# Experts 4 to 6 stored from 96 partitions in 16 KB runs, and the last expert's output moved into a used weight slot

## The chip, the cores and the metric

The kernel runs on one core of one Trainium2 chip. The metric is the device time of one execution in microseconds (us); smaller is better. The engines are named as in the profile: PE is TensorE, DVE is VectorE, ACT is ScalarE, POOL is GpSimd and SP is SyncE. PEld is PE's weight load. The core has 16 DMA engines, which move data between HBM (device memory) and SBUF (on-chip memory of 128 partitions) for whichever engine issues the transfer. The kernel issues transfers from two engines: POOL, whose queue the profile calls q0, and SP, whose queue it calls q1.

## The reference

Eight experts each apply a two-layer network with a ReLU to 256 rows of their own. Inputs and output are float32.

```python
n_experts, capacity, hidden, expert_hidden = 8, 256, 512, 2048
# x: [8, 256, 512]   w1: [8, 512, 2048]   w2: [8, 2048, 512]
def reference(x, w1, w2):
    h = np.matmul(x, w1)
    h = np.maximum(h, 0)
    return np.matmul(h, w2).astype(np.float32)
```

The two weights of one expert are 4 MB each, so 64 MB of weights are read once; x is 4 MB and the output is 4 MB (512 KB for each expert).

## The kernel before, in words

**Loads.** All weights are loaded by POOL (line 204), in the order of the list `loads`: w1 and w2 of experts 0 and 1 together, of 2 and 3 together, then w1 of 4 and 5 together, and after that w2 of 4 and 5 and both weights of 6 and 7 one by one. The last w2 comes in two pieces, of 1280 KB and 768 KB in bfloat16. The loads convert float32 to bfloat16 on the way. There are four slots for w1 and four for w2 (`NS = 4`), so expert 4 uses the slots of expert 0, and so on; POOL waits for PE to be done with a slot before it issues the load that refills it. Everything on q0 is worked off in the order of issue, and each weight transfer lands tens of microseconds after it was issued.

**Start.** x comes in two parts: its first half through SP into `out_sb` (which holds no output yet) and its second half through POOL. PE transposes x in 64 steps (`xt_ps`), and DVE and ACT copy the transposed blocks out of PSUM into `xT` (`copy_xt`, lines 223 and 227): one copy for the columns of experts 0 to `QE` - 1 (the "early" ones, whose rows are put into another order, see below) and one for the rest (the "late" ones). `QE` is 4.

**Experts.** For each expert PE makes 64 matmuls of the first layer in four groups into two PSUM tiles (`h_ps`); ACT applies the ReLU and writes bfloat16 (`hT`, line 269). Then 32 matmuls of the second layer go into one PSUM tile `o_ps` of two halves. DVE copies `o_ps` to `out_sb`. PE may not write `o_ps` again before that, so DVE counts up the semaphore `c_o` twice for each expert, and PE takes one count near the end of each half of the next expert's first layer.

**Outputs of experts 0 to 3.** The rows of these experts are ordered so that 32 partitions hold one expert, eight rows of 512 numbers each. DVE copies `o_ps` in four pieces of 32 partitions x 1024 numbers (line 244), each onto the 32 partitions of its expert. `out_sb` then holds on each of 128 partitions a run of 16 KB that is also 16 KB in one piece in HBM.

**Outputs of experts 4 to 7.** DVE copies the two halves as they are, 128 partitions x 512 numbers (line 255); the second half of the last expert is copied by ACT (line 275). A partition then holds 4 KB for each expert, and 4 KB is what lies in one piece in HBM.

**Stores.** There are three. POOL waits until DVE is done with expert 6 (`s_event`) and until the piece of 1280 KB of the last w2 has landed (`landed[-2]`), and then issues the store of experts 4 to 6 (line 207: 1536 KB, 128 partitions x 3 runs of 4 KB) and that of experts 0 to 3 (line 210: 2048 KB, 128 runs of 16 KB). SP waits for both copies of the last expert (`v_last`) and issues its store (line 166: 512 KB, 128 runs of 4 KB). The kernel ends when all have landed.

Of the kernel before, what the change touches and what calls it, by code (L numbers as in the profile page):

```python
# [8 lines left out]
FP32 = mybir.dt.float32  # L9
# [7 lines left out]
def kernel(  # L17
# [7 lines left out]
    nc = tc.nc  # L25
    P = 128
    E, C, H = x.shape
    F = w1.shape[2]
    MC = C // P
# [3 lines left out]
    R = E * C // P  # L33
# [20 lines left out]
    out_v = out.rearrange("e (p mo) k -> p e (mo k)", mo=MC)  # L54
# [4 lines left out]
    def allot(name, shape, dtype):  # L59
        nonlocal free  # L60
        places[name] = free
        t = nc.alloc_sbuf_tensor_at(name, shape, dtype, offset=free)
        free += math.prod(shape[1:]) * mybir.dt.size(dtype)
        return t


    out_sb = allot("out_sb", [P, E, MC, H], FP32)
    w1_sb = allot("w1_sb", [P, NS, K1 * F], BF16)
    w2_sb = allot("w2_sb", [P, NS, K2 * H], BF16)
    xT = allot("xT", [P, K1, MC, E * P], BF16)  # L70
    hT = allot("hT", [P, K2, C], BF16)
    identity = allot("identity", [P, P], BF16)
    W1_AT, W2_AT, XT_AT = places["w1_sb"], places["w2_sb"], places["xT"]
# [4 lines left out]
    xt_ps = [nc.alloc_psum_tensor(f"xt_ps{i}", [P, R // MC, P], BF16) for i in range(MC)]  # L78
    h_ps = [nc.alloc_psum_tensor(f"h_ps{i}", [P, GJ * C], FP32) for i in range(UG)]
    o_pair = nc.alloc_psum_tensor("o_ps", [P, MC * H], FP32)  # L80
    o_ps = [o_pair[:, i * H:(i + 1) * H] for i in range(MC)]
# [3 lines left out]
    def sem(name):  # L85
        s = nc.alloc_semaphore(name)
        sems.append(s)
        return s

    d_last, d_pool = sem("d_last"), sem("d_pool")  # L90
# [7 lines left out]
    s_event, s_cast, s_stored = sem("s_event"), sem("s_cast"), sem("s_stored")  # L98
    s_pe, v_last = sem("s_pe"), sem("v_last")
# [10 lines left out]
    def after_outputs(e, halves):  # L110
        return s_pe, K1 * MC + e * (NG + MC) + NG + halves


    c_h, c_o, c_w1, c_w2 = sem("c_h"), sem("c_o"), sem("c_w1"), sem("c_w2")
# [15 lines left out]
    for w, es, h, _ in loads:  # L130
        s = d_half if h else d_w[w, es[0] % NS]
# [4 lines left out]

    QE = 4
    G = P // QE
    out_q = out_sb[:, :QE].rearrange("p e m h -> p (e m h)")
    out_qv = out[:QE].rearrange("e (p s) k -> (e p) (s k)", s=QE * MC)  # L140

    x_head = out_sb[:, :HEAD // MC].rearrange("p e m h -> p (e m h)")

# [17 lines left out]
    sp = nc.sync  # L161
    for i, (w, es, h, n) in enumerate(loads):
        sp.wait_ge(*landed[i])
        sp.sem_inc((c_w1, c_w2)[w - 1], n * len(es) if w == 2 else len(es))
    sp.wait_ge(v_last, MC)
    sp.dma_start(
        out_v[:, E - 1, :], out_sb[:, E - 1].rearrange("p m h -> p (m h)")
    ).then_inc(d_last, 16)
    sp.sem_inc(s_stored, 1)
    take(sp, d_last, 16)  # L170

# [1 line left out]
    pool = nc.gpsimd  # L173
# [5 lines left out]
        out=identity[:],  # L179
# [7 lines left out]
    for i, (w, es, h, n) in enumerate(loads):  # L187
# [10 lines left out]
        e, ne, at_slot = es[0], len(es), es[0] % NS  # L198
# [3 lines left out]
        else:  # L202
            src, dst = w1_v[:, e:e + ne, :], w1_sb[:, at_slot:at_slot + ne, :]
        pool.dma_start(dst, src).then_inc(landed[i][0], 16)  # L204
    pool.wait_ge(s_event, 3)
    pool.wait_ge(*landed[-2])
    pool.dma_start(  # L207
        out_v[:, QE:E - 1, :], out_sb[:, QE:E - 1].rearrange("p e m h -> p e (m h)")
    ).then_inc(d_pool, 16)
    pool.dma_start(out_qv, out_q).then_inc(d_pool, 16)  # L210
    pool.wait_ge(s_stored, 1)
    pool.wait_ge(d_pool, 48)
    used = [s.num for s in sems[1:]]
# [4 lines left out]


    def copy_xt(copy, ko, m):  # L220
        split = QE * C // R
        early, late = xT[:, ko, m, :QE * P], xT[:, ko, m, QE * P:]
        copy(  # L223
            early.rearrange("k (e g i hi) -> k hi g e i", e=QE, g=QE, hi=2),
            xt_ps[m][:, :, :split].rearrange("k (hi g) (e i) -> k hi g e i", hi=2, e=QE),
        )
        return copy(  # L227
            late.rearrange("k (ep r2) -> k ep r2", r2=R // MC),
            xt_ps[m][:, :, split:].rearrange("k r2 ep -> k ep r2"),
        )  # L230


    dve = nc.vector
# [3 lines left out]
    for ko in range(K1):  # L237
        dve.wait_ge(*after_transposes(ko * MC + 1))
        copy_xt(dve.tensor_copy, ko, 0).then_inc(c_xt[0])
    dve.sem_inc(c_o, MC)  # L240
    for e in range(QE):
        dve.wait_ge(*after_outputs(e, MC))
        for g in range(QE):
            cp = dve.tensor_copy(  # L244
                out_q[e * G:(e + 1) * G, g * MC * H:(g + 1) * MC * H],
                o_pair[g * G:(g + 1) * G, :],
            )
            if g >= QE - MC:
                cp.then_inc(c_o)
    for e in range(QE, E):  # L250
        for m in range(MC):
            if e == E - 1 and m == 1:
                break
            dve.wait_ge(*after_outputs(e, m + 1))
            cp = dve.tensor_copy(out_sb[:, e, m, :], o_ps[m])  # L255
            cp.then_inc(v_last if e == E - 1 else c_o)
        if e == E - 2:
            dve.drain().then_inc(s_event)


    act = nc.scalar
    act.sem_inc(c_xt[1], 1)
    for ko in range(K1):
        act.wait_ge(*after_transposes(ko * MC + 2))
        copy_xt(act.copy, ko, 1).then_inc(c_xt[1])
# [6 lines left out]
                mybir.ActivationFunctionType.Relu,  # L272
            ).then_inc(c_h)
    act.wait_ge(*after_outputs(E - 1, MC))
    act.copy(out_sb[:, E - 1, 1, :], o_ps[1]).then_inc(v_last)  # L275

# [50 lines left out]
    n = MC * (R // MC)  # L329
# [47 lines left out]
    lo, hi = bank  # L377
# [129 lines left out]
```

## Time and profile before

| | |
|---|---|
| median of 3 runs | 178.95 us (178.81 to 178.97) |
| the profiled execution, its own time | 178.98 us |
| its span, from the first to the last instruction or transfer | 177.7 us |
| PE busy | 128.1 us, 72% of the span |
| DVE busy, ACT busy | 31.6 us, 39.3 us |
| HBM read and written | 71.30 MB, 4.19 MB |

The profile is of one execution. Its own time is 1.28 us more than its span; times inside it are counted from the span's start. "Landing" of a transfer is the time from its issue until its semaphore shows that all of it has arrived. In the line of transferred GB/s, bytes are counted as they are written, so a load that converts float32 to bfloat16 shows half of what it reads.

### The profile page before, as it was taken

The page shows a single profiled execution, that of the slowest core. Times are in us where ns is not written, and L with a number is a line of the kernel's source. Part 1 is how long each engine was busy: PE and PEld are TensorE (multiplying, and loading weights), DVE is VectorE, ACT ScalarE, POOL GpSimd, SP SyncE. Part 2 cuts the span into 40 slices and gives each one's busy share as a digit, 9 for nine tenths or more (in the row PEclk, how much of TensorE's full clock was granted, in tenths as well). Part 3 has the DMA queues.
Part 4 walks back from the last instruction along what each step waited for, and adds up shares of the span by engine and source line. Part 5 has one row for each costly group of instructions (what it writes and reads, how often), then busy time and mean ns, then how long its engine had stood idle before and what let it go on. Part 6 is the DMA issues. An engine that isn't in the chain of part 4 may idle for free. (4 is left out here: it accounts for less than half of the span.)

```text
span 177.7 us, 2092 instructions
## 1 busy us (share of the span) xinstructions
PE 128.1 (72%) x832; PEld 89.4 (50%) x832; DVE 31.6 (18%) x32; ACT 39.3 (22%) x42; POOL 10.0 (6%) x21
## 2 busy tenths in 40 slices
PE   0008620793039989989069989989999999979980
PEld 0007520592013587488024885686497488459530
DVE  0054420000000180082000640280020020020010
ACT  2002520054000044025100242044035026005310
POOL 3400010000000002010000101200000000000200
PEclk9999999999756999999858999999999999999998
DMA  5999989989999999999999999999999999999998
GB/s 201 358 212 232 236 184 229 236 188 225 236 196 218 236 196 218 236 203 210 236 203 210 236 207 207 236 207 207 236 207 207 236 207 207 236 200 203 286 440 347
DMA packets 3488, 40.90 MB, mean 230 GB/s; under 512 B 288, under 2 KB 288, under 8 KB 928
## 3 DMA queue, kind: packets, MB, share of 16 engines
q0 software_dynamic: 3056, 38.27, 96.4%
q1 hardware_dynamic: 432, 2.62, 3.8%
HBM read 71.30 MB, written 4.19 MB: 425 GB/s over the span
## 5 line engine op out<-in xcount | busy, mean ns | idle before, releaser
L305 PE MATMUL o_ps<-w_sb,hT 128*128 x256 | 61.0, 399 | 16.7 <-PEq L102 16.7
L305 PE MATMUL h_ps<-xT,w_sb 128*128 x512 | 61.2, 279 | 11.8 <-PEq L102 11.8
L305 PEld LDWEIGHTS h_ps<-xT,w_sb 128*128 x512 | 57.4, 145 | 16.6 <-issue 14.1
L269 ACT ACTIVATE hT<-h_ps 128x1024 bf16<-128x1024 f32 x32 | 32.8, 1024 | 109.2 <-PE h_ps L305 109.2
L305 PEld LDWEIGHTS o_ps<-w_sb,hT 128*128 128x128 bf16 x256 | 25.5, 102 | 49.4 <-issue 23.0
L244 DVE COPY out_sb<-o_ps 32x1024 f32<-32x1024 f32 x16 | 19.5, 1220 | 75.8 <-PE o_ps L305 75.6
L305 PE MATMUL xt_ps<-identity,w_sb 128*128 128x128 bf16 x64 | 7.6, 312 | 15.8 <-PEq L102 15.8
L305 PEld LDWEIGHTS xt_ps<-identity,w_sb 128*128 x64 | 6.5, 147 | 16.6 <-issue 16.6
L255 DVE COPY out_sb<-o_ps 128x512 f32<-128x512 f32 x7 | 4.6, 687 | 49.2 <-PE o_ps L305 49.2
L204 POOL DMA_DIRECT2D w_sb<-in_w_dram x12 | 7.3, 615 | 103.9 <-PE h_ps L305 59.7
L223 ACT COPY xT<-xt_ps 128x512 bf16<-128x512 bf16 x4 | 2.9, 719 | 16.2 <-PE xt_ps L305 16.2
L235 DVE CAST w_sb<-out_sb 128x4096 bf16<-128x4096 f32 x1 | 2.3, 2295 | 10.4 <-DMA out_sb<-in_x_dram 10.4
L223 DVE COPY xT<-xt_ps 128x512 bf16<-128x512 bf16 x4 | 2.9, 730 | 5.9 <-PE xt_ps L305 5.9
L207 POOL DMA_DIRECT2D out_dram<-out_sb x1 | 0.8, 754 | 49.1 <-DMA w_sb<-in_w_dram 49.1
L227 DVE COPY xT<-xt_ps 128x512 bf16<-128x512 bf16 x4 | 2.7, 674 | 0.0
L227 ACT COPY xT<-xt_ps 128x512 bf16<-128x512 bf16 x4 | 2.4, 588 | 0.0
L275 ACT COPY out_sb<-o_ps 128x512 f32<-128x512 f32 x1 | 0.6, 586 | 5.9 <-PE o_ps L305 5.9
L223 ACT ACT_TABLE_LOAD x1 | 1.3, 1283 | 2.5 <-PEq L159 2.5
L174 POOL DMA_DIRECT2D w_sb<-in_x_dram x1 | 0.7, 650 | 2.5 <-POOLq L159 2.5
L210 POOL DMA_DIRECT2D out_dram<-out_sb x1 | 0.6, 572 | 0.0
L178 POOL TENSOR_SCALAR_AFFINE_SELECT identity<-identity 128x128 bf16<-128x128 bf16 x1 | 0.3, 282 | 0.2 <-POOL identity L175 0.2
L175 POOL MEMSET identity<- 128x128 bf16 x1 | 0.2, 223 | 0.0
(4 smaller groups left out, 0.4 us busy)
## 6 DMA issues: line engine op xcount, KB each, us to landing
w_sb<-in_w_dram POOLq DMA_DIRECT2D x5, 4096.0 KB, 46.3
w_sb<-in_w_dram POOLq DMA_DIRECT2D x5, 2048.0 KB, 50.4
out_sb<-in_x_dram SPq DMA_DIRECT2D x2, 1024.0 KB, 7.0
out_dram<-out_sb POOLq DMA_DIRECT2D x1, 2048.0 KB, 11.0
out_dram<-out_sb POOLq DMA_DIRECT2D x1, 1536.0 KB, 6.8
w_sb<-in_w_dram POOLq DMA_DIRECT2D x1, 1280.0 KB, 49.6
w_sb<-in_x_dram POOLq DMA_DIRECT2D x1, 1024.0 KB, 9.9
w_sb<-in_w_dram POOLq DMA_DIRECT2D x1, 768.0 KB, 52.7
```

The costliest lines, as they stand in the source:

```text
L174: pool.dma_start(x_sb[:, HEAD * H:], x_v[:, HEAD * H:]).then_inc(d_pool, 16)
L204: pool.dma_start(dst, src).then_inc(landed[i][0], 16)
L207: pool.dma_start(out_v[:, QE:E - 1, :], out_sb[:, QE:E - 1].rearrange("p e m h -> p e (m h)")).then_inc(d_pool, 16)
L210: pool.dma_start(out_qv, out_q).then_inc(d_pool, 16)
L223: copy(early.rearrange("k (e g i hi) -> k hi g e i", e=QE, g=QE, hi=2), xt_ps[m][:, :, :split].rearrange("k (hi g) (e i) -> k hi g e i", h ...
L227: return copy(late.rearrange("k (ep r2) -> k ep r2", r2=R // MC), xt_ps[m][:, :, split:].rearrange("k r2 ep -> k ep r2"),)
L235: dve.tensor_copy(x_sb[:, :HEAD * H], x_head).then_inc(s_cast)
L244: cp = dve.tensor_copy(out_q[e * G:(e + 1) * G, g * MC * H:(g + 1) * MC * H], o_pair[g * G:(g + 1) * G, :],)
L255: cp = dve.tensor_copy(out_sb[:, e, m, :], o_ps[m])
L269: act.activation(hT[:, g * GJ:(g + 1) * GJ, :].rearrange("p a c -> p (a c)"), h_ps[g % UG][:], mybir.ActivationFunctionType.Relu,).then_in ...
L275: act.copy(out_sb[:, E - 1, 1, :], o_ps[1]).then_inc(v_last)
L305: return pe.add_instruction(inst)
```

## The change

The 16 KB runs are extended from the first four to the first seven experts (`QA = 7`).

- DVE copies the outputs of experts 4 to 6 in four pieces of 32 x 1024 each, as it did those of 0 to 3, onto partitions 0 to 95 and behind the run of experts 0 to 3. Partitions 96 to 127 stay empty there. The two counts of `c_o` are given after the second and the fourth piece (before: after the third and the fourth), for all seven experts.
- `copy_xt` treats the columns of seven experts as early and those of the last one as late.
- POOL's two stores trade places: experts 0 to 3 first, now behind `landed[-2]` and a `s_event` that DVE gives after expert 3, then experts 4 to 6 behind a second `s_event` that DVE gives after expert 6. The latter is 96 runs of 16 KB on 96 partitions, in place of 384 runs of 4 KB on 128.
- The last expert's output goes to `last_sb`, which lies where the first w1 slot is (that of experts 0 and 4).

```diff
     QE = 4
     G = P // QE
-    out_q = out_sb[:, :QE].rearrange("p e m h -> p (e m h)")
-    out_qv = out[:QE].rearrange("e (p s) k -> (e p) (s k)", s=QE * MC)
+    QA = E - 1
+    out_q = out_sb.rearrange("p e m h -> p (e m h)")
+    out_qv = out.rearrange("e (p s) k -> (e p) (s k)", s=QE * MC)
+    RUN = QE * MC * H
+    last_sb = nc.alloc_sbuf_tensor_at("last_sb", [P, MC, H], FP32, offset=W1_AT)
...
-    pool.wait_ge(s_event, 3)
     pool.wait_ge(*landed[-2])
-    pool.dma_start(
-        out_v[:, QE:E - 1, :], out_sb[:, QE:E - 1].rearrange("p e m h -> p e (m h)")
-    ).then_inc(d_pool, 16)
-    pool.dma_start(out_qv, out_q).then_inc(d_pool, 16)
+    for first in range(0, QA, QE):
+        n = (min(first + QE, QA) - first) * G
+        at_run = first // QE * RUN
+        pool.wait_ge(s_event, 3 + first // QE)
+        pool.dma_start(
+            out_qv[first * G:first * G + n, :], out_q[:n, at_run:at_run + RUN]
+        ).then_inc(d_pool, 16)
...
-    for e in range(QE):
+    for e in range(QA):
         dve.wait_ge(*after_outputs(e, MC))
         for g in range(QE):
+            at_run = e // QE * RUN + g * MC * H
             cp = dve.tensor_copy(
-                out_q[e * G:(e + 1) * G, g * MC * H:(g + 1) * MC * H],
+                out_q[e % QE * G:(e % QE + 1) * G, at_run:at_run + MC * H],
                 o_pair[g * G:(g + 1) * G, :],
             )
-            if g >= QE - MC:
+            if g % MC == MC - 1:
                 cp.then_inc(c_o)
-    for e in range(QE, E):
-        for m in range(MC):
-            if e == E - 1 and m == 1:
-                break
-            dve.wait_ge(*after_outputs(e, m + 1))
-            cp = dve.tensor_copy(out_sb[:, e, m, :], o_ps[m])
-            cp.then_inc(v_last if e == E - 1 else c_o)
-        if e == E - 2:
+        if e in (QE - 1, QA - 1):
             dve.drain().then_inc(s_event)
+    dve.wait_ge(*after_outputs(E - 1, 1))
+    dve.tensor_copy(last_sb[:, 0, :], o_ps[0]).then_inc(v_last)
...
-    act.copy(out_sb[:, E - 1, 1, :], o_ps[1]).then_inc(v_last)
+    act.copy(last_sb[:, 1, :], o_ps[1]).then_inc(v_last)
```

On POOL, the end of its program stood like this before (a name before the arrow is written, the one behind it is read; w_sb are the weight slots, d_w2_3 is the semaphore of `landed[-2]`):

```order
L204 DMA w_sb<-in_w_dram 128x8192 [waits s_pe] x5
L204 DMA w_sb<-in_w_dram 128x5120 [waits s_pe]
L204 DMA w_sb<-in_w_dram 128x3072
L207 DMA out_dram<-out_sb 128x3x1024 [waits d_w2_3,s_event]
L210 DMA out_dram<-out_sb 128x4096
L216 ISA [waits d_pool,s_stored]
```

And it stands like this with the change:

```order
L205 DMA w_sb<-in_w_dram 128x8192 [waits s_pe] x5
L205 DMA w_sb<-in_w_dram 128x5120 [waits s_pe]
L205 DMA w_sb<-in_w_dram 128x3072
L211 DMA out_dram<-out_sb 128x4096 [waits s_event,d_w2_3]
L211 DMA out_dram<-out_sb 96x4096 [waits s_event]
L219 ISA [waits d_pool,s_stored]
```

The store of experts 0 to 3 has moved ahead of that of 4 to 6, and the latter has 96 runs of 4096 numbers instead of 128 x 3 runs of 1024 and a wait of its own.

On DVE, the end of its program, from expert 2 on, stood like this before (o_ps is the PSUM tile of the second layer):

```order
L244 COPY out_sb<-o_ps 32x1024 [waits s_pe]
L244 COPY out_sb<-o_ps 32x1024 x3
L244 COPY out_sb<-o_ps 32x1024 [waits s_pe]
L244 COPY out_sb<-o_ps 32x1024 x3
L255 COPY out_sb<-o_ps 128x512 [waits s_pe] x7
```

And from expert 4 on it stands like this with the change:

```order
L248 COPY out_sb<-o_ps 32x1024 [waits s_pe]
L248 COPY out_sb<-o_ps 32x1024 x3
L248 COPY out_sb<-o_ps 32x1024 [waits s_pe]
L248 COPY out_sb<-o_ps 32x1024 x3
L248 COPY out_sb<-o_ps 32x1024 [waits s_pe]
L248 COPY out_sb<-o_ps 32x1024 x3
L257 COPY last_sb<-o_ps 128x512 [waits s_pe]
```

Six of the seven copies of 128 x 512 have become twelve of 32 x 1024, with one wait for each expert instead of one for each half.

## Rows read from the trace of the kernel before

**Rows 1.** The page: busy time, DMA in 40 slices, queues, bytes.

```profile
PE 128.1 (72%) x832; PEld 89.4 (50%) x832; DVE 31.6 (18%) x32; ACT 39.3 (22%) x42; POOL 10.0 (6%) x21
...
DMA  5999989989999999999999999999999999999998
...
q0 software_dynamic: 3056, 38.27, 96.4%
q1 hardware_dynamic: 432, 2.62, 3.8%
HBM read 71.30 MB, written 4.19 MB: 425 GB/s over the span
```

**Rows 2.** Chain that ended last: start us, us, what.

```profile
158.14 0.04 issue
158.18 7.31 PE h_ps L305 x64
165.49 6.97 PE o_ps L305 x32
172.46 0.02 issue
172.48 0.59 ACT out_sb L275
```

**Rows 3.** Timeline, end: start us, us, engine, line; [idle before <-releaser].

```profile
157.05 1.29 DVE L255 COPY out_sb<-o_ps 128x512 f32<-128x512 f32 x2 [12.79 <-PE o_ps L305]
...
158.18 7.31 PE L305 MATMUL h_ps<-xT,w_sb 128*128 x64 [0.95 <-PEq L102]
...
164.70 0.75 POOL L207 DMA_DIRECT2D out_dram<-out_sb  x1 [49.12 <-DMA w_sb<-in_w_dram]
...
165.45 0.57 POOL L210 DMA_DIRECT2D out_dram<-out_sb  x1
...
173.10 0.35 SPq L166 DMA_DIRECT2D out_dram<-out_sb  x1
```

**Rows 4.** Transfers by issue: engine, count, KB each, us from issue to landing.

```profile
out_dram<-out_sb POOLq DMA_DIRECT2D x1, 2048.0 KB, 11.0
out_dram<-out_sb POOLq DMA_DIRECT2D x1, 1536.0 KB, 6.8
...
w_sb<-in_w_dram POOLq DMA_DIRECT2D x1, 768.0 KB, 52.7
out_dram<-out_sb SPq DMA_DIRECT2D x1, 512.0 KB, 4.5
```

**Rows 5.** Line 204, the weight loads: first and last issue, time to landing.

```profile
L204 POOL DMA_DIRECT2D w_sb<-in_w_dram x12: 528/554/733, 4.5 to 115.0; - x12
...
DMA to landing us min/median/max: 27.7/50.0/66.6
```

**Rows 6.** Four stretches; the last three columns: granted clock, DMA share, GB/s.

```profile
100.00:150.00 50.00, 49.03 (x346) 36.50 (x345) 11.78 (x12) 15.36 (x15) 1.80 (x4) 1.00 1.01 215
...
167.50:170.50 3.00, 3.00 (x15) 1.37 (x14) 0.00 (x0) 0.00 (x0) 0.00 (x0) 1.00 1.03 423
171.50:175.50 4.00, 0.95 (x5) 0.22 (x3) 0.69 (x1) 0.59 (x1) 0.00 (x0) 1.00 1.00 430
176.50:177.50 1.00, 0.00 (x0) 0.00 (x0) 0.00 (x0) 0.00 (x0) 0.00 (x0) 0.50 0.49 197
```

**Rows 7.** Timeline around expert 4's first layer, where DVE copies expert 3.

```profile
114.06 3.55 PE L305 MATMUL h_ps<-xT,w_sb 128*128 x31
114.27 4.95 DVE L244 COPY out_sb<-o_ps 32x1024 f32<-32x1024 f32 x4 [9.90 <-PE o_ps L305]
...
118.10 4.02 PE L305 MATMUL h_ps<-xT,w_sb 128*128 x33 [0.49 <-PEq L102]
```

**Rows 8.** Groups of instructions by line: DVE's copies; count | busy us, mean ns | idle before.

```profile
L244 DVE COPY out_sb<-o_ps 32x1024 f32<-32x1024 f32 x16 | 19.5, 1220 | 75.8 <-PE o_ps L305 75.6
...
L255 DVE COPY out_sb<-o_ps 128x512 f32<-128x512 f32 x7 | 4.6, 687 | 49.2 <-PE o_ps L305 49.2
L223 DVE COPY xT<-xt_ps 128x512 bf16<-128x512 bf16 x4 | 2.9, 730 | 5.9 <-PE xt_ps L305 5.9
...
L227 DVE COPY xT<-xt_ps 128x512 bf16<-128x512 bf16 x4 | 2.7, 674 | 0.0
```

**Rows 9.** Timeline of the start: POOL's fourth load, last copy_xt, first expert.

```profile
23.67 0.72 POOL L204 DMA_DIRECT2D w_sb<-in_w_dram  x1 [17.02 <-PE xt_ps L305]
23.99 0.59 ACT L227 COPY xT<-xt_ps 128x512 bf16<-128x512 bf16 x1
...
32.34 9.08 PE L305 MATMUL h_ps<-xT,w_sb 128*128 x64 [8.97 <-PEq L102]
```

More of the change, by code (lines that the diff above doesn't have):

```diff
@@ L165 @@
     sp.wait_ge(v_last, MC)
-    sp.dma_start(
-        out_v[:, E - 1, :], out_sb[:, E - 1].rearrange("p m h -> p (m h)")
-    ).then_inc(d_last, 16)
+    sp.dma_start(out_v[:, E - 1, :], last_sb.rearrange("p m h -> p (m h)")).then_inc(d_last, 16)
     sp.sem_inc(s_stored, 1)
@@ L220, in copy_xt @@
     def copy_xt(copy, ko, m):
-        split = QE * C // R
-        early, late = xT[:, ko, m, :QE * P], xT[:, ko, m, QE * P:]
+        split = QA * C // R
+        early, late = xT[:, ko, m, :QA * P], xT[:, ko, m, QA * P:]
         copy(
-            early.rearrange("k (e g i hi) -> k hi g e i", e=QE, g=QE, hi=2),
-            xt_ps[m][:, :, :split].rearrange("k (hi g) (e i) -> k hi g e i", hi=2, e=QE),
+            early.rearrange("k (e g i hi) -> k hi g e i", e=QA, g=QE, hi=2),
+            xt_ps[m][:, :, :split].rearrange("k (hi g) (e i) -> k hi g e i", hi=2, e=QA),
         )
```

## The prediction, made before the change was run

> **What bounds the kernel now.** I read the page first. PE is busy 72% of the span, DVE 18%, ACT 22%, but the DMA line stands at 8 or 9 tenths from the second slice to the last, and q0 alone, the queue of the weights and of POOL's two stores, fills 96.4% of the time of all 16 engines [rows 1]. So the kernel is a stream of bytes, and every part of the change has to be asked first what it does to that stream.
>
> The chain of waits then shows only the end: last expert's first layer from 158.18, second layer, ACT's copy until 173.07 [rows 2]. The timeline shows that this chain starts with a wait of 0.95 us (for w1 of expert 7, the last thing that PE lacked) and what comes behind it: POOL issues its two stores at 164.70 and 165.45, SP the last one at 173.10 [rows 3]. From issue and landing I work out when the transfers follow each other. The last piece of weights is issued at 115.0 and lands 52.7 later, at 167.7 [rows 4, 5]. The 1536 KB store lands at 164.70 + 6.8 = 171.5, the 2048 KB store at 165.45 + 11.0 = 176.45, SP's at 173.10 + 4.5 = 177.6 [rows 3, 4], which is the end of the span. They arrive one behind the other: 3.8 us for the first, 4.95 for the second, 1.15 for SP's. SP issued 3.35 us before POOL's second store had landed, and its 512 KB needed only 1.15 us more after that (at 430 GB/s 512 KB take 1.22 us). So SP's store is waiting for the engines, not they for it. The end of the kernel is therefore the end of POOL's two stores plus about 1.15 us, and the PE chain has some slack against it.
>
> **The change part by part.** The sum is made against the profiled execution: 178.98 us, of which the span is 177.7; the median of the runs is 178.95, 0.03 lower.
>
> *Start, copy_xt.* DVE's two copies of 512 columns take 730 and 674 ns [rows 8], together 1404. With 7/8 and 1/8 of the columns, and if all of the time goes with the columns, they take 730 x 1.75 + 674 x 0.25 = 1446 ns; if none does, 1404. That is 0 to 0.04 us for each of four steps, at most 0.17 us later at the end of the transposes. The last copy ends at 24.58 and PE starts the first layer at 32.34, when the weights are there [rows 9]: 7.8 us of cover. Without that cover it would cost the 0.17 us. POOL's load at 23.67 waits for the transposes too [rows 9] and would be issued up to 0.17 us later; weight loads land 27.7 to 66.6 us after their issue, with a stream in front of them that never breaks [rows 1, 5], so it costs nothing.
>
> *DVE, experts 4 to 6.* Four copies of 1220 ns instead of two of 687 ns [rows 8]: 4.9 us instead of 1.3 us for each expert. For experts 0 to 3 this is so already: there DVE starts 0.21 us after PE's next first layer and takes 4.95 us, and PE stands 0.49 us at the end of its first half, since the first count comes only after the third piece (3.7 us) while PE is there after 3.55 us [rows 7]. The count now comes after the second piece, at 0.2 + 2.4 = 2.6 us, so these waits go; the second count comes at 0.2 + 4.9 = 5.1 us, when PE has need of it at some 7.1 us. The gain of 0.49 us in four places is worth nothing: PE waits for weights anyway, 0.95 us before the last expert [rows 3]. The copies of expert 6 would end at about 157.3 + 4.95 = 162.2. POOL's second wait is for that, and POOL doesn't come to its first store before 164.70 [rows 3], so 2.5 us of cover; nothing else is queued behind that wait but the end of the kernel.
>
> *The last expert.* `last_sb` lies in a slot whose weights expert 4 used last; the copies have the same shapes, and SP's store too. Zero.
>
> *Order of the stores.* 2048 KB then 1536 KB instead of the reverse: the same queue, the same gate (the 1280 KB piece), the same bytes before SP's. Zero by itself.
>
> *The runs: 96 of 16 KB instead of 384 of 4 KB.* This is the one term on the path. What longer runs can give is to be seen by comparing the stretches in which one store has the engines: 423 GB/s with 4 KB runs, 430 with 16 KB [rows 6]. 1.573 MB take 3.72 us at the one and 3.66 at the other; by the landings, 3.8 against 0.75 x 4.95 = 3.71. So the gain is 0.06 to 0.09 us, if the rate holds.
>
> What 96 partitions cost, the trace does not show: all its transfers lie on 128. I bound it from two sides. If the rate belongs to the 16 engines and 96 rows are dealt out 6 to each, the store takes 3.7 us: **-0.1 us**. If the rate belongs to the partitions, that is, if a group of 8 partitions has one sixteenth of it, then the busiest group still has 8 rows of 16 KB, and the store takes as long as the one of 128 rows, 4.95 us: 4.95 - 3.8 = **+1.15 us**. To be done in 3.7 us, 96 partitions would have to give 1.573 MB at 425 GB/s, 4.4 GB/s each; the most that the trace has of any is 430/128 = 3.4 GB/s each, in the stores, and loads put only 215 GB/s into SBUF [rows 6]. The nearest row is the 2048 KB store: same queue, same run, with 32 partitions less. I take its time, 4.95 us, and keep both ends.
>
> [...]
>
> **The sum.** POOL's second store lands 1.15 us later, at 177.6, SP's at 178.75, and the time is 178.98 + 1.15 = 180.1 us.
>
> **The rivals.**
>
> *A. Engines share evenly, no loss.* For it: loads and stores come to the same rate (215 GB/s written from twice as many bytes read, 430 stored [rows 6]), as if the engines were the limit and not the partitions. Against it: in the loads SBUF gets half of that, and only the stores could show its limit; they show no rate above 430. Then -0.1 us, 178.9: no change that can be measured. (About 0.2%, 0.36 us, is what a measurement of this kernel can tell from none.) It decides if the store of 96 rows lands under 4.2 us after the other one.
> [...]
>
> *B. Worse than by groups.* If the rows are dealt out 6 to an engine and two engines meet on the same group of partitions, some wait for each other, and the last engine ends later than the balanced 4.95 us. Worst by the rows: all 6 rows at half rate, 2 x 3.7 = 7.4 us, +3.6 us, 182.6. For it: nothing in the trace, since 128 rows give each of 16 engines 8 rows without any meeting. Against it: early engines would leave the groups to the late ones.
>
> *C. Faster.* The store of 4 KB runs costs more than I see, because the issue of 384 runs takes POOL 0.75 us against 0.57 for 128 [rows 3] and the short runs cost 0.1 us of rate. 0.18 + 0.1 = 0.28 us, and with some of SP's store moved beside POOL's where an engine is done early, 0.4 us: 178.6. Against it: the second issue is over at 166.02, before the last weights land at 167.7, so POOL's issue is hidden; and the last engine sets the end.
>
> *D. DVE becomes late.* If the copies of expert 6 ended after 172 (when the first store is through), POOL's second store would stand. It needs 10 us more than worked out; I give it no chance of its own.
>
> **How the numbers follow.** The store at the rate of partitions, 180.1 (+0.8 to +1.6, that is 179.8 to 180.6): 0.4. Rival B, 180.6 to 182.6: 0.2. Rival A, 178.7 to 179.3: 0.35. Rival C: 0.05. Slower by over 0.2% is the first two, 0.6; same is A, 0.35; faster is C, 0.05. The range goes from 178.7, which takes in all of A, to 181.8, which leaves out the worst third of B and most of C, some 0.1 together; the likeliest case's own range is 179.8 to 180.6.
>
> **What would show it.** In the list of transfers POOL's store of 1536 KB should land 4.9 us or more behind that of 2048 KB, and SP's 1.1 to 1.2 us behind that or less. The rate should fall clearly below 430 GB/s from about 172.6 on, to some 320 on the mean of that store, and not before. The waits of 0.49 us on PE should be gone, and expert 7 should still start at 158.2. The prediction is wrong if the rate stays at 420 to 430 while the 96 rows go out (then A), and its size is wrong if the store takes over 6 us (then B). It is wrong in its first part if SP's store ends at the old time although POOL's ends later, since I hold that SP's bytes are behind POOL's on every engine.

## The result, and the profile after

The changed kernel takes 180.98 us (median of 6 runs, 180.36 to 182.87) against 178.94 (6 runs, 178.81 to 179.01): 2.04 us more, a ratio of 1.0124 with a 95% interval of 1.0077 to 1.0171. It is slower, as forecast, and inside the range, but the loss is nearer to two than to the one that I had predicted. The runs also lie 2.5 us apart where those of before lie 0.2. The profiled execution is the fastest of the six, 180.36 us with a span of 179.0, so what it shows is the small end of the loss.

The transfers by issue, with KB and us from issue to landing, answer to [rows 4]:

```profile
out_dram<-out_sb POOLq DMA_DIRECT2D x1, 2048.0 KB, 8.3
out_dram<-out_sb POOLq DMA_DIRECT2D x1, 1536.0 KB, 12.9
...
out_dram<-last_sb SPq DMA_DIRECT2D x1, 512.0 KB, 5.9
```

The timeline of the end, as in [rows 3], and the line of POOL's two stores, whose last field is the first and the last issue:

```profile
156.28 4.94 DVE L248 COPY out_sb<-o_ps 32x1024 f32<-32x1024 f32 x4 [9.14 <-PE o_ps L304]
...
158.20 7.32 PE L304 MATMUL h_ps<-xT,w_sb 128*128 x64 [1.96 <-PEq L102]
...
173.12 0.35 SPq L169 DMA_DIRECT2D out_dram<-last_sb  x1
```

```profile
L211 POOL DMA_DIRECT2D out_dram<-out_sb x2: 525/531/537, 164.3 to 164.9; - x2
```

The store of experts 0 to 3 lands at 164.35 + 8.3 = 172.65, that of 4 to 6 at 164.9 + 12.9 = 177.8, SP's at 173.12 + 5.9 = 179.0. The views round landings to 0.1 us, so a difference of two landings is good to some 0.1 us. The 1536 KB took 5.15 us, where the kernel before needed 3.8 us for the same bytes; SP's store followed 1.2 us later, as before. PE's last expert still starts at 158.2, SP still issues at 173.1: all of the loss is in the store.

The rate in stretches, with the columns of [rows 6] (the last three are granted clock, DMA share, GB/s):

```profile
167.50:170.50 3.00, 3.00 (x16) 1.37 (x14) 0.00 (x0) 0.00 (x0) 0.00 (x0) 1.00 1.02 437
172.70:174.70 2.00, 0.00 (x0) 0.00 (x0) 0.28 (x1) 0.39 (x1) 0.00 (x0) 1.00 0.94 360
174.70:176.70 2.00, 0.00 (x0) 0.00 (x0) 0.00 (x0) 0.00 (x0) 0.00 (x0) 1.00 0.98 311
176.70:178.70 2.00, 0.00 (x0) 0.00 (x0) 0.00 (x0) 0.00 (x0) 0.00 (x0) 0.67 0.39 156
```

437 GB/s while 128 partitions are stored, 360 and then 311 while 96 are (SP's last 512 KB, issued at 173.12, may be among the bytes of the latter stretch). The DMA share stays at 0.94 and 0.98: the engines count as busy, but move less. A DMA share of 0.98 stood beside 311 GB/s here, one of 1.02 beside 437.

PE's part went as worked out. Around expert 4's first layer the timeline has one piece of 64 matmuls where [rows 7] has two with 0.49 us between them, and DVE's copies cost the same:

```profile
113.85 7.29 PE L304 MATMUL h_ps<-xT,w_sb 128*128 x64
114.05 4.95 DVE L248 COPY out_sb<-o_ps 32x1024 f32<-32x1024 f32 x4 [9.13 <-PE o_ps L304]
```

About half of the four waits' time came back as a longer wait for the last expert's weights, 1.96 us instead of 0.95. PE reached expert 4 only 0.21 us earlier (113.85 against 114.06), and its granted clock before that was lower than in the profile of before. The stretch from 84 to 98 us, first before, then with the change:

```profile
84.00:98.00 14.00, 7.60 (x27) 3.09 (x28) 0.00 (x0) 1.02 (x1) 0.53 (x1) 0.76 0.98 208
```

```profile
84.00:98.00 14.00, 7.62 (x24) 2.93 (x25) 0.00 (x0) 0.00 (x0) 0.00 (x0) 0.63 0.98 209
```

That is a difference between two executions and not the work of the change: two kernels of the experiments that are alike up to then (0 to 63 and 32 to 95 below) show 0.76 and 0.63 there as well.

### The profile page after: what moved, and what is told of

It reads as the page before. It is cut to its first block, busy times and chain, and to the rows that moved or that the text cites. A ratio compares the mean times of both kernels' runs of the same rounds, so it can differ in the third digit from the quotient of the medians.

```text
span 179.0 us, 2099 instructions
## 1 busy us (share of the span) xinstructions
PE 126.9 (71%) x832; PEld 89.4 (50%) x832; DVE 42.4 (24%) x38; ACT 39.7 (22%) x42; POOL 9.8 (5%) x21
## 3 DMA queue, kind: packets, MB, share of 16 engines
q1 hardware_dynamic: 432, 2.62, 3.8%
## 5 line engine op out<-in xcount | busy, mean ns | idle before, releaser
L248 DVE COPY out_sb<-o_ps 32x1024 f32<-32x1024 f32 x28 | 34.2, 1220 | 103.2 <-PE o_ps L304 102.7
L226 ACT COPY xT<-xt_ps 128x896 bf16<-128x896 bf16 x4 | 4.6, 1142 | 15.9 <-PE xt_ps L304 15.9
L226 DVE COPY xT<-xt_ps 128x896 bf16<-128x896 bf16 x4 | 4.6, 1146 | 6.5 <-PE xt_ps L304 6.5
L257 DVE COPY last_sb<-o_ps 128x512 f32<-128x512 f32 x1 | 0.7, 692 | 11.1 <-PE o_ps L304 11.1
L274 ACT COPY last_sb<-o_ps 128x512 f32<-128x512 f32 x1 | 0.6, 585 | 5.9 <-PE o_ps L304 5.9
L230 DVE COPY xT<-xt_ps 128x128 bf16<-128x128 bf16 x4 | 1.1, 273 | 0.0
L230 ACT COPY xT<-xt_ps 128x128 bf16<-128x128 bf16 x4 | 1.1, 268 | 0.0
## 6 DMA issues: line engine op xcount, KB each, us to landing
out_dram<-out_sb POOLq DMA_DIRECT2D x1, 1536.0 KB, 12.9
```

The costliest lines, as they stand in the source:

```text
L226: copy(early.rearrange("k (e g i hi) -> k hi g e i", e=QA, g=QE, hi=2), xt_ps[m][:, :, :split].rearrange("k (hi g) (e i) -> k hi g e i", h ...
L230: return copy(late.rearrange("k (ep r2) -> k ep r2", r2=R // MC), xt_ps[m][:, :, split:].rearrange("k r2 ep -> k ep r2"),)
L248: cp = dve.tensor_copy(out_q[e % QE * G:(e % QE + 1) * G, at_run:at_run + MC * H], o_pair[g * G:(g + 1) * G, :],)
L257: dve.tensor_copy(last_sb[:, 0, :], o_ps[0]).then_inc(v_last)
L274: act.copy(last_sb[:, 1, :], o_ps[1]).then_inc(v_last)
```

## The experiments

Two theories stood against each other, with the rest of the change as a third. *Partitions*: groups of partitions have their own share of the rate, so 96 of them leave a group as full as 128 do. *Engines*: the rate belongs to the 16 engines, and the loss is something else (dealing 6 rows to an engine, long runs, addresses in HBM). *The rest*: order of the stores, copies, the last expert's place.

**All of the change but the layout.** From the kernel before, with the two stores in the new order, the earlier count and `last_sb`:

```diff
+    pool.wait_ge(s_event, 3)
+    pool.dma_start(out_qv, out_q).then_inc(d_pool, 16)
+    pool.wait_ge(s_event, 4)
     pool.dma_start(
         out_v[:, QE:E - 1, :], out_sb[:, QE:E - 1].rearrange("p e m h -> p e (m h)")
     ).then_inc(d_pool, 16)
-    pool.dma_start(out_qv, out_q).then_inc(d_pool, 16)
...
-            if g >= QE - MC:
+            if g % MC == MC - 1:
```

> All of the change but the layout of experts 4 to 6: the two stores trade places, the earlier count for PE, the last expert's output in the weight slot; experts 4 to 6 stay in 4 KB runs on 128 partitions. Theory (the 96 partitions cost the time): 178.9 to 179.1 us, the same as before, with the 1536 KB store landing 3.8 us behind the 2048 KB one. Rival (the order of the stores or one of the other edits costs it): 180 to 181 us.

Measured 179.00 us, ratio 1.0007 (0.9997 to 1.0017): no change. Its stores by issue, and the issues:

```profile
out_dram<-out_sb POOLq DMA_DIRECT2D x1, 2048.0 KB, 8.4
out_dram<-out_sb POOLq DMA_DIRECT2D x1, 1536.0 KB, 11.6
```

```profile
164.34 0.54 POOL L209 DMA_DIRECT2D out_dram<-out_sb  x1 [49.30 <-DMA w_sb<-in_w_dram]
164.87 0.75 POOL L211 DMA_DIRECT2D out_dram<-out_sb  x1
```

Landings at 172.74 and 176.47: 3.7 us for 1536 KB from 128 partitions. The third theory is out; the loss needs the 96 partitions.

**Fewer bytes, from 96 partitions.** The kernel before, with one store cut:

```diff
-        out_v[:, QE:E - 1, :], out_sb[:, QE:E - 1].rearrange("p e m h -> p e (m h)")
+        out_v[:96, QE:E - 1, :], out_sb[:96, QE:E - 1].rearrange("p e m h -> p e (m h)")
```

> The kernel before, with its store of experts 4 to 6 cut to partitions 0 to 95 (1152 KB instead of 1536 KB, 4 KB runs as before; a quarter of the rows of experts 4 to 6 is not stored). Theory (the rate belongs to groups of partitions, and the busiest group has its full 24 runs): no gain from a quarter fewer bytes, 178.9 to 180.0 us. Rival (the rate belongs to the engines, which share 288 runs evenly): 0.25 x 3.8 = 0.95 us less, 178.0 us. Rival (only 16 KB runs suffer): 178.0 us as well.

Measured 179.88 us (179.07 to 180.81), ratio 1.0050 (1.0028 to 1.0073): a quarter of that store is left out, and the kernel is slower. The last weights land at 115.8 + 52.0 = 167.8, the cut store at 164.87 + 7.7 = 172.57, 4.8 us for 1152 KB, where the kernel before took 3.8 for 1536 KB:

```profile
out_dram<-out_sb POOLq DMA_DIRECT2D x1, 1152.0 KB, 7.7
...
w_sb<-in_w_dram POOLq DMA_DIRECT2D x1, 768.0 KB, 52.0
```

```profile
L204 POOL DMA_DIRECT2D w_sb<-in_w_dram x12: 528/552/723, 4.5 to 115.8; - x12
```

```profile
164.87 0.69 POOL L207 DMA_DIRECT2D out_dram<-out_sb  x1 [48.48 <-DMA w_sb<-in_w_dram]
```

The runs are of 4 KB here, so the loss doesn't need the long runs.

**More bytes, from 128 partitions.** The changed kernel, with its second store replaced:

```diff
-        pool.dma_start(
-            out_qv[first * G:first * G + n, :], out_q[:n, at_run:at_run + RUN]
-        ).then_inc(d_pool, 16)
+        dst = out_qv[:P, :] if first == 0 else spare
+        pool.dma_start(dst, out_q[:, :RUN]).then_inc(d_pool, 16)
```

> The changed kernel, but its second store sends the runs of experts 0 to 3 from all 128 partitions once more, to a spare tensor (2048 KB in 128 runs of 16 KB; experts 4 to 6 are not stored). Theory (partitions): 8 rows for each group and no meeting, 4.95 us behind the first store, total 178.95 + 1.15 = 180.1 us: a third more bytes than the changed kernel's 1536 KB and yet faster than its 180.98. Rival (bytes through the engines, with a loss of another kind that goes with the second store): 1.2 us more than the changed kernel, 182.2 us.

Measured 180.07 us (180.02 to 180.14), as the theory of partitions had it: a third more bytes than in the changed kernel and 0.9 us less. The second store lands 164.80 + 12.8 - (164.27 + 8.3) = 5.0 us behind the first, and the four runs are within 0.12 us:

```profile
out_dram<-out_sb POOLq DMA_DIRECT2D x1, 2048.0 KB, 8.3
spare<-out_sb POOLq DMA_DIRECT2D x1, 2048.0 KB, 12.8
```

**Which partitions.** The same 1024 KB (experts 4 and 5, 64 runs of 16 KB, the same addresses in HBM, 4 rows to an engine if they are dealt evenly to the 16) from three places in SBUF; for partitions 32 to 95:

```diff
-            out_qv[first * G:first * G + n, :], out_q[:n, at_run:at_run + RUN]
+            out_qv[first * G:first * G + n, :], out_q[at:at + n, at_run:at_run + RUN]
...
+            q = (e + (e >= QE) * 1) % QE
             cp = dve.tensor_copy(
-                out_q[e % QE * G:(e % QE + 1) * G, at_run:at_run + MC * H],
+                out_q[q * G:(q + 1) * G, at_run:at_run + MC * H],
```

Here `at` is 0 and `n` is 128 for the first store, and 1 x `G` and 64 for the second; with 0 or 2 in place of 1 the experts lie on partitions 0 to 63 or 64 to 127.

Partitions 0 to 63: 

> The changed kernel with PE's count as before (after the third and fourth piece) and its second store cut to experts 4 and 5 on partitions 0 to 63 (1024 KB in 64 runs of 16 KB, 4 to an engine; expert 6 is not stored). Theory (a partition and the one 32 further on are in each other's way when rows of both are sent at once): far more than the 2.43 us that 64 rows of partitions 32 to 95 took in the split kernel, up to 4.95 us, so up to 180.1 us with a third less to store. Rival (the loss comes from dealing 6 rows to an engine, or from the addresses in HBM): 2.5 us, the end set by SP's store alone, 177.6 us.

Partitions 32 to 95: 

> As the kernel with partitions 0 to 63, with experts 4 and 5 on partitions 32 to 95 instead: same bytes, same addresses in HBM, same runs, same number to an engine (expert 6 is not stored). Theory (partitions 32 apart): 2.45 us, 177.6 us. Rival (the number of partitions or the dealing matters, not which): as the kernel with partitions 0 to 63.

Partitions 64 to 127: 

> The changed kernel with its earlier count, its second store cut to experts 4 and 5 on partitions 64 to 127 (1024 KB, 64 runs of 16 KB; expert 6 is not stored). [...] Rival (it is partitions 0 to 31 that are slow, for whatever reason): 2.43 us, and 177.5 us.

Partitions 32 to 95 with the earlier count: 

> As the kernel with partitions 64 to 127, on 32 to 95 (expert 6 is not stored). With the later count, PE stood 0.48 us three times more, in the first layers of experts 5 to 7, and SP issued its store only at 175.02. Theory (that was what kept it at 178.76): the store takes 2.43 us again, SP issues at 173.1 and the time is 177.5 us. Rival (SP's own store sets a floor, whatever is stored ahead of it): 178.7 us again.

The times were 180.07, 178.76, 180.02 and 177.78 us (the kernel before, run beside them, 179.04 for the first two and 178.95 for the others). The lines of the 1024 KB store and its issue, in this order: 0 to 63,

```profile
out_dram<-out_sb POOLq DMA_DIRECT2D x1, 1024.0 KB, 12.5
```

```profile
L213 POOL DMA_DIRECT2D out_dram<-out_sb x2: 533/536/539, 164.4 to 165.0; - x2
```

64 to 127,

```profile
out_dram<-out_sb POOLq DMA_DIRECT2D x1, 1024.0 KB, 12.1
```

```profile
L213 POOL DMA_DIRECT2D out_dram<-out_sb x2: 535/536/537, 164.3 to 164.9; - x2
```

and 32 to 95 with the earlier count:

```profile
out_dram<-out_sb POOLq DMA_DIRECT2D x1, 1024.0 KB, 10.2
```

```profile
L213 POOL DMA_DIRECT2D out_dram<-out_sb x2: 512/524/537, 164.3 to 164.9; - x2
```

The 2048 KB store lands 8.3 us after the first issue in all three. So the 1024 KB took 164.98 + 12.5 - (164.44 + 8.3) = 4.7 us from 0 to 63, 164.87 + 12.1 - (164.33 + 8.3) = 4.3 us from 64 to 127, and 164.87 + 10.2 - (164.33 + 8.3) = 2.4 us from 32 to 95 (the second issue comes some 0.54 us, one issue's duration, after the first). In the 2 us after 172.7 the rate was 221 GB/s from 0 to 63 and 246 from 64 to 127:

```profile
172.70:174.70 2.00, 0.62 (x3) 0.10 (x1) 0.69 (x1) 0.59 (x1) 0.00 (x0) 1.00 1.00 221
```

```profile
172.70:174.70 2.00, 1.27 (x6) 0.39 (x4) 0.69 (x1) 0.59 (x1) 0.00 (x0) 1.00 1.05 246
```

That is a little over half of 430, with a DMA share of 1.00 and more. Only where the rows lie in SBUF differs, so the loss comes neither from the addresses in HBM, nor from the number of partitions, nor, if the dealing is the same each time, from that of rows to an engine. The 64 rows that all lie in partitions 0 to 63, or all in 64 to 127, went out at about half the rate (1.049 MB in 4.7 and 4.3 us, 223 and 244 GB/s), and those spread evenly over both halves at the full one (in 2.4 us, 437 GB/s; the trace has 373 in the 2 us after 172.7). Whether a row is slowed only by one 32 partitions away, or by any other of its half, these four runs do not tell. With 64 to 127, 4.3 us rule out the 2.43 of the rival that has only partitions 0 to 31 slow; but the 180.02 us are not the store's alone, since SP issued late, at 174.62, for the reason in the last section.

The forecast of 177.6 for 32 to 95 failed at first (178.76): SP issued only at 175.02. There are two reasons. With the later count DVE's four pieces made PE stand 0.48 us in the first layers of experts 5 to 7 also; that was of my making. But the kernel with 0 to 63 has the same count, and its SP issued at 173.97. The other 1.0 us were there by expert 4, which PE began at 114.85 against 113.82, behind a stretch with a lower granted clock. The stretch from 84 to 98 us, first with 0 to 63, then with 32 to 95:

```profile
84.00:98.00 14.00, 7.53 (x28) 3.16 (x29) 0.00 (x0) 0.78 (x1) 0.53 (x1) 0.76 1.00 213
```

```profile
84.00:98.00 14.00, 7.67 (x23) 2.93 (x24) 0.00 (x0) 0.14 (x1) 0.00 (x0) 0.63 0.98 208
```

With the earlier count PE came to expert 6 as late as in the profile of the change, which has 0.63 there (142.08 us against 142.00), but it then still waited 1.86 us for the last expert's weights, and SP issued at 173.11: 177.78 us against 177.5 forecast. Its seven runs lie in two groups, 177.65 to 177.78 and 178.49 to 178.67, and only one of the first group was profiled, so what the second one waited for is not known.

**96 partitions in pieces.** The store of the changed kernel issued as two, partitions 32 to 95 and then 0 to 31 (for the three pieces the list is `[(0, G), (G, 2 * G), (2 * G, n)]`):

```diff
+        for a, b in [(0, n)] if n == P else [(G, n), (0, G)]:
+            pool.dma_start(
+                out_qv[first * G + a:first * G + b, :], out_q[a:b, at_run:at_run + RUN]
+            ).then_inc(d_pool, 16)
```

Two pieces: 

> The changed kernel with its store of 96 partitions issued as two: partitions 32 to 95 first, then 0 to 31. All outputs are stored. [...] Rival (engines share evenly, the loss is one of a single odd-sized transfer): 178.9 us. Rival (one more transfer costs more): over 181 us.

Two pieces, PE's count as before: 

> The split kernel (partitions 32 to 95, then 0 to 31) with PE's count as before. All outputs are stored. Theory (the two stores took 3.8 us as the 4 KB runs did, and the 0.75 us that the split kernel was over the kernel before came from PE, whose clock was low in expert 7's first layer after a wait of 2.66 us): PE waits less, the clock stays up, 178.9 to 179.0 us. Rival (the split itself costs it): 179.7 us again.

Three pieces, PE's count as before: 

> The changed kernel with PE's count as before and its store of 96 partitions issued as three, of partitions 0 to 31, 32 to 63 and 64 to 95. All outputs are stored. Theory in its second form (only rows of two blocks of 32 that are sent at once are in each other's way; 32 rows of one block took 1.36 us in the split kernel): 3 x 1.3 = 3.9 us, 178.9 to 179.2 us. [...] Rival (the loss goes with the 96 rows in whatever form): 181 us.

Two pieces gave 179.69 us (179.36 to 179.93). The stores and their issues:

```profile
out_dram<-out_sb POOLq DMA_DIRECT2D x1, 2048.0 KB, 8.3
...
out_dram<-out_sb POOLq DMA_DIRECT2D x1, 1024.0 KB, 10.2
...
out_dram<-out_sb POOLq DMA_DIRECT2D x1, 512.0 KB, 11.1
out_dram<-last_sb SPq DMA_DIRECT2D x1, 512.0 KB, 3.2
```

```profile
L212 POOL DMA_DIRECT2D out_dram<-out_sb x3: 499/512/537, 164.6 to 165.6; - x3
```

Partitions 32 to 95 took 2.4 us again, 0 to 31 only 1.4 us (165.6 + 11.1 = 176.7, behind 175.3), where half of the 4.7 us for 0 to 63 would be 2.35. So the same 96 rows took 3.8 us in two pieces, and 5.15 in one. SP issued only at 174.96 here, for the reason in the last section, so the 179.69 us are not those of the stores alone. From the 1.4 us I took it that 32 partitions of one block are not slowed, and forecast 178.9 to 179.2 for three pieces. That was wrong: 182.49 us (182.22 to 183.04). The line of its four stores shows landings from 8.3 to 13.7 us after the issue, and the transfers by issue show the median of the three blocks, which is the second one's:

```profile
L212 POOL DMA_DIRECT2D out_dram<-out_sb x4: 489/502/537, 164.4 to 165.9; - x4
...
DMA to landing us min/median/max: 8.3/10.3/13.7
```

```profile
out_dram<-out_sb POOLq DMA_DIRECT2D x3, 512.0 KB, 11.2
```

From 164.42 + 8.3 = 172.7 to 165.9 + 13.7 = 179.6 the three blocks took 6.9 us, but not in equal parts. The second landed at 165.45 + 11.2 = 176.65, so 0 to 31 and 32 to 63 took 3.9 us together, less than the 4.7 that they took as one store of 64 rows, and 64 to 95 took 3.0, more than half of the 4.3 for 64 to 127. SP had issued its store at 174.03, and its rows may have gone out beside those of the third block. So half the rate for every block, 3 x 2.35 = 7.05 us by the store of 0 to 63 (an estimate), fits the sum and not block by block. Three stores of one block each were slow in all, so the loss doesn't need rows 32 partitions apart in one store. Whether a block alone is slowed, or only because its rows overlap in time with those of the block before, these runs do not separate, and why the single block behind 32 to 95 shows 1.4 us is not settled.

With the later count two pieces gave 179.98 us, not the 178.9 forecast. POOL's last store landed at 176.8, some 0.35 us later than in the kernel before, but SP issued only at 174.81, again for the three waits of 0.48 us and a late PE ahead of them (it began expert 6 at 144.33 us, against 143.49 with 0 to 63). So this run does not tell what the split costs with PE undisturbed, and that stays open.

**A version that follows.** 16 KB runs for experts 4 and 5 on partitions 32 to 95, 4 KB runs on 128 partitions for expert 6:

```diff
+    pool.dma_start(out_qv[P:P + 2 * G, :], out_q[G:3 * G, RUN:]).then_inc(d_pool, 16)
+    pool.dma_start(out_v[:, QA, :], six_sb.rearrange("p m h -> p (m h)")).then_inc(d_pool, 16)
```

> A version that follows from the runs so far: 16 KB runs for six experts, the fifth and sixth of them on partitions 32 to 95, and expert 6 in 4 KB runs on 128 partitions as before; the earlier count for PE is kept. All outputs are stored. Theory (no two blocks 32 apart in one store): 2.43 us for experts 4 and 5 and 8 x 0.158 = 1.27 us for expert 6, 3.7 us against 3.8 before: 178.85 us, 0.1 us under the kernel before and hardly to be told from it. Rival (what the long runs on fewer than 128 partitions cost is not gone): 179.5 us or more.

Measured 178.93 us against 178.95, ratio 0.9999 (0.9990 to 1.0008). The loss is gone, and there is no gain. POOL's stores and SP's:

```profile
out_dram<-out_sb POOLq DMA_DIRECT2D x1, 2048.0 KB, 8.4
...
out_dram<-out_sb POOLq DMA_DIRECT2D x1, 1024.0 KB, 10.3
...
out_dram<-six_sb POOLq DMA_DIRECT2D x1, 512.0 KB, 11.0
out_dram<-last_sb SPq DMA_DIRECT2D x1, 512.0 KB, 4.5
```

## Why the prediction was right, and where its size was off

*The bound.* Right: SP's store ended 1.2 us behind POOL's, which was 1.15 before, and all other edits together were worth nothing (179.00 us without the layout).

*copy_xt, DVE, PE.* Right. DVE's two copies took 1146 + 273 = 1419 ns, between the 1404 and 1446 worked out. The copies of expert 6 ended at 161.2, 3.1 us ahead of POOL's first store. The four waits of 0.49 us went, and nothing came of it.

```profile
L226 DVE COPY xT<-xt_ps 128x896 bf16<-128x896 bf16 x4 | 4.6, 1146 | 6.5 <-PE xt_ps L304 6.5
...
L230 DVE COPY xT<-xt_ps 128x128 bf16<-128x128 bf16 x4 | 1.1, 273 | 0.0
```

*What long runs give.* 0.06 to 0.09 us by the rows of before; the last version, which has them without the loss, could not be told from the kernel before.

*What 96 partitions cost.* The choice between the two ends was right: what the store costs goes by which partitions its rows lie on, and not by bytes or engines alone. This is shown by the same bytes from three places (4.7, 4.3, 2.4 us) and by 1152 KB that took longer than 1536 KB. One reason given for it was wrong: 3.4 GB/s is not the most that a partition gives, since the 64 of 32 to 95 gave 1.049 MB in 2.4 us, 6.8 GB/s each. That a group of eight partitions has a sixteenth of the rate was an assumption of mine, and no run shows it; groups of eight neighbours are out, for then 32 to 95 would have taken 4.95 us and not 2.4. A fixed half of the 430 GB/s for partitions 0 to 63 and another for 64 to 127, 215 each, is an estimate that roughly fits the runs with 64 rows, 221 and 246 GB/s. It doesn't fit the store in two pieces: 0 to 31 sent 512 KB in 1.4 us, some 375 GB/s, and the 96 rows took 3.8 us where 1.049 MB from 0 to 63 at 215 GB/s want 4.9. So a fixed share is not the whole account, and what is missing stays open.

*The size.* The term "as long as the store of 128 rows, 4.95 us" was too small. The profiled execution shows 5.15 us and is 1.4 us over the one of before, but the median is 2.04 us over. That is rival B's interval (180.6 to 182.6), not the likeliest case's (179.8 to 180.6): 4.95 us, the time of the 2048 KB store, was an estimate for the busiest group, and the 96 rows took longer than that. The store's 5.15 us are under the 6 that the prediction had as the sign of B; no slower run was profiled. The four runs with 128 rows, where each of the assumed groups has 8, lie within 0.12 us, the six with 96 within 2.5, the eight with the cut store within 1.7. That engines meet at a group in an order that changes from run to run would explain this; the profile doesn't show which engine reads which row, so it is only argued. I should have given B more weight than 0.2, since I had no reason why an uneven load should balance itself. The range also left out two fifths of B's interval (181.8 to 182.6 of 180.6 to 182.6), not a third. The median lies inside it; the slowest of the six runs, 182.87, doesn't.

## What to carry to other kernels

Look at which partitions a store's rows lie on, not only at how many there are. In these runs, by the landings, stores from 128 partitions (1536 KB in 3.7 to 3.8 us, 414 to 425 GB/s), or from 32 to 95 (437), had the full rate, and single stores from 0 to 63 (223), 64 to 127 (244) or 0 to 95 (1536 KB in 5.15 us, 305) did not. Before runs are made longer at the price of fewer partitions, compare the rate of the runs as they are: 423 GB/s with 4 KB against 430 with 16 KB left 0.1 us to win and over a microsecond to lose. Here, where the DMA engines set the end, what PE saved only made its wait for the last weights longer (1.96 us for 0.95), and in two kernels the wait had a price of its own, as the next section shows.

## What the runs showed of the hardware that I had not expected

In two kernels PE's granted clock fell right behind the wait for the last weights, which the earlier count had made longer (0.95 us before, 1.96 with the change). In the kernel with two pieces PE waited 2.66 us before expert 7. The clock was still 1.00 in that wait and 0.53 on the mean of the next 3.6 us; the first layer took 8.93 us instead of 7.3, and SP issued at 174.96:

```profile
158.43 8.93 PE L305 MATMUL h_ps<-xT,w_sb 128*128 x64 [2.66 <-PEq L102]
```

```profile
155.80:158.30 2.50, 0.00 (x0) 0.00 (x0) 2.45 (x3) 0.00 (x0) 0.00 (x0) 1.00 0.81 170
158.40:162.00 3.60, 3.57 (x18) 2.89 (x19) 2.34 (x2) 0.00 (x0) 0.00 (x0) 0.53 1.08 228
```

The same was seen after 2.62 us in the kernel with partitions 64 to 127 (a clock of 0.54 in the next 3.5 us, 8.86 us for the layer), so its 180.02 us is not the store's alone. After waits of 1.85 to 2.25 us, in five of the other kernels, the layer took 7.3 us. So a wait that is free for the DMA engines was followed by 1.6 us more of PE's time in these two kernels, to be set against what slack SP's store has there.
